# A decoder layer on one core: the last head's scaling on ScalarE, the residual rows on SP's queue, the first up weight's low parts on VectorE, the second up weight's splits moved within the token chains

## The chip, the core and the metric

The kernel runs on one core of one Trainium2 chip. The core has five engines that work side by side, each through its own instructions in order: TensorE (PE, matmuls), VectorE (DVE), ScalarE (ACT), GpSimd (POOL), and SyncE (SP), which here only issues DMAs. ACT issues DMAs too, and such an issue stands in ACT's queue like any other instruction. The metric is the device time of one execution in microseconds (us).

## What is computed

One layer of a decoder, for 512 tokens of 1024 numbers, in float32. Cut to what matters here:

```python
u = rms_norm(x, mix_pre_g) * (1.0 + sc1) + sh1        # sh, sc, g: six rows from cond @ ada_w + ada_b
h = mlstm_chunkwise(...)                              # 4 heads x 256
h = rms_norm(h, ml_norm_g) * sigmoid(o_pre)           # per head
y = silu(layer_norm(causal_dwconv(a * sigmoid(gt))))  # convolution group
mix = jnp.concatenate([h, y], axis=-1) @ w_out
x = x + g1 * rms_norm(mix, mix_post_g)
u = rms_norm(x, ffn_pre_g) * (1.0 + sc2) + sh2
up = causal_dwconv(u @ ffn_up)                        # 2 x 2816 columns
a, gt = jnp.split(up, 2, axis=-1)
f = (silu(gt) * a) @ ffn_down
x = x + g2 * rms_norm(f, ffn_post_g)
```

## The kernel before

Every large product is made of three matmuls (`mm3`): each operand is split into a high part, rounded by a copy on ACT (L191), and a low part, the difference, by a subtraction on POOL or DVE (L192). `w_split` does this for one 128x512 piece of a weight, `w_load` for a whole load of 1 MB, which is four pieces. Weights come through two buffers (`raws`, RAWS = 2): SP can issue a load only when the splits of the load before last have read their buffer. Split pieces live in `wpool` (20 tiles, ten pieces) or in `slots`.

The order on PE and SP is that of the program. ACT, DVE and POOL are ordered by a scheduler, except inside `in_order()`, where they too run in program order. The queue of each engine is then fixed: an instruction that waits holds up all behind it.

The part of the program that the change touches runs from the last head's attention to the first up products:

- **The last head** (`attention(3)`). For each of four token tiles PE makes a bank `o`; ACT reads from it the denominator (`dm`, L545), copies it to `hn` (L546) and sums its squares (L547). Then DVE and POOL make four columns `rd` and `fac` (L552 to L557), DVE scales the four pieces of `hn` by both (L560), PE transposes them (`hT`, L566), and DVE and ACT make from them the high and low parts `hh`, `hl` that the output projection reads.
- **The first half of the output projection** (`mix_first`, banks `mixa`), of which 10 of 16 steps stand ahead of hT and 6 behind it, and then the first 8 steps of the second half (banks `mixb`, one for each token tile).
- **The modulation** (`ada_block`, L174 to L176). Loads of 512 KB on ACT's queue, each multiplied and summed by DVE. Sixteen of them run behind the last head, through six buffers (four in `spare`, two in `adas`). They end in `gains` (L931 to L933), which PE transposes (`gT`, L665); DVE copies the result to `gTs` (L667), and SP sends it to memory and reads it back as rows for all partitions (`gs2r`, `sh2r`).
- **The residual** `x1`: eight tiles of x, 256 KB each, loaded on ACT's queue (L921) into buffers that the convolution group has used.
- **The token chains**, inside `in_order()` (L1013 to L1049). For each token tile: `mix_last` ends its `mixb` bank; `chain_sums` squares it on ACT, multiplies it on DVE (L948) and makes a factor on DVE and POOL; `chain_x` adds it to `x1` (L955), squares the sum and makes the next factor; `chain_u` ends the normalised tile `un` (L963); `turn_tile` transposes it on PE (`xT`, L971); `turn_out` splits it into `u2h`, `u2l`. Then come the first products of the feed-forward part (`up_half`). Between these steps stand single pieces of the second and third up weight (`up_split`), whose low parts are made on DVE.

The names in the views: `wo` is a piece of the output weight, `wup` one of an up weight, and `wup_0`, `_512`, `_1024`, `_1536` are its four pieces; `h` and `l` at the end are the high and the low part.

Of the kernel before, what the change touches and what calls it, by code (L numbers as in the profile page):

```python
# [13 lines left out]
AF = mybir.ActivationFunctionType  # L14
ALU = mybir.AluOpType
# [4 lines left out]
T = 512  # L20
KT = D // P
NT = T // P
H = 4
# [32 lines left out]
def decoder_layer(ctx, tc, w_glu0, x, c, adaT, vecs, w_glu, w_qko, w_v0, w_v, w_out, w_up, w_down, out):  # L56
    nc = tc.nc
    V, S, G, PE = nc.vector, nc.scalar, nc.gpsimd, nc.tensor

    const = ctx.enter_context(tc.tile_pool(name="const", bufs=1))  # L60
    slots = ctx.enter_context(tc.tile_pool(name="slots", bufs=SLOTS))
# [123 lines left out]
    def w_split(src, name, pool=None, tag="w", eng=None):  # L185

        n = src.shape[1]
        pool = pool or wpool
        hi = pool.tile([P, T], F32R, tag=tag, name=f"{name}h")
        lo = pool.tile([P, T], F32R, tag=tag, name=f"{name}l")  # L190
        S.activation(hi[:, :n], src, AF.Copy)  # L191
        (eng or G).tensor_tensor(out=lo[:, :n], in0=src, in1=hi[:, :n].bitcast(F32), op=ALU.subtract)  # L192
        return hi, lo

    def w_load(view, name, pool=None, tag="w"):

        n = view.shape[1]
        r = raws.tile([P, 2048], F32, tag="raw", name=name)
        nc.sync.dma_start(r[:, :n], view)
        return [w_split(r[:, a : min(a + T, n)], f"{name}_{a}", pool, tag) for a in range(0, n, T)]  # L200

    def blk(pieces, b):
        hi, lo = pieces[b // 4]
# [109 lines left out]
    _, _, u = u_tiles("u")  # L313
# [209 lines left out]
    def attention(h):  # L523

        _, qs, ks, so = heads[h]

        for cc in range(NT):
            n = NS[cc]
            sp = atbank(f"s{h}_{cc}")
            for d in range(2):  # L530
                PE.matmul(sp[:, :n], ks[d][:, cc * P : (cc + 1) * P], qs[d][:, cc * P :], start=d == 0, stop=d == 1)  # L531
            last_e[0] = V.scalar_tensor_tensor(out=E[h][cc], in0=sp[:, :n], scalar=DH**-0.5, in1=E[h][cc], op0=ALU.mult, op1=ALU.mult)
            if cc in ((0, 2, 3) if h == 0 else (1, 3)):
                yield
        ssq = small.tile([P, NT], F32, tag="ssq", name=f"ssq{h}")
        dm = small.tile([P, NT], F32, tag="dm", name=f"dm{h}")
        hn = [slot(f"hn{h}_{i}") for i in range(2)]
        for tt in range(NT):
            o = atbank(f"o{h}_{tt}")
            for cc in range(tt + 1):  # L540
                a = (tt - cc) * P
                PE.matmul(o[:, : DH + 2], E[h][cc][:, a : a + P], vs[h][cc], start=cc == 0, stop=cc == tt)  # L542
            junk = small.tile([P, DH], BF16, tag="junk2", bufs=1, name=f"junko{h}_{tt}")
            hv = hn[tt // 2][:, (tt % 2) * DH : (tt % 2 + 1) * DH]
            S.activation(dm[:, tt : tt + 1], o[:, DH : DH + 1], AF.Abs)  # L545
            S.activation(hv, o[:, :DH], AF.Copy)  # L546
            S.activation(junk, hv, AF.Square, accum_out=ssq[:, tt : tt + 1])  # L547
            if tt in (1, 2):
                yield
        rd = small.tile([P, NT], F32, tag="rd", name=f"rd{h}")  # L550
        fac = small.tile([P, NT], F32, tag="fac", name=f"fac{h}")
        V.tensor_tensor(out=dm, in0=dm, in1=em[:, :, h], op=ALU.max)  # L552
        V.reciprocal(rd, dm)
        V.scalar_tensor_tensor(out=ssq, in0=ssq, scalar=1.0 / DH, in1=rd, op0=ALU.mult, op1=ALU.mult)
        V.tensor_tensor(out=ssq, in0=ssq, in1=rd, op=ALU.mult)
        G.tensor_scalar(out=ssq, in0=ssq, scalar1=EPS, scalar2=None, op0=ALU.add)
        G.tensor_tensor(out=fac, in0=ssq, in1=mhalf, op=ALU.pow)  # L557
        for tt in range(NT):
            hv = hn[tt // 2][:, (tt % 2) * DH : (tt % 2 + 1) * DH]
            V.tensor_scalar(out=hv, in0=hv, scalar1=fac[:, tt : tt + 1], scalar2=rd[:, tt : tt + 1], op0=ALU.mult, op1=ALU.mult)  # L560
        yield
        for e in range(2):
            tp = atbank(f"hT{h}_{e}")
            for tt in range(NT):
                src = hn[tt // 2][:, (tt % 2) * DH + e * P : (tt % 2) * DH + (e + 1) * P]
                PE.transpose(tp[:, tt * P : (tt + 1) * P], src, ident)  # L566
            t = so[e]
            V.scalar_tensor_tensor(out=t, in0=t, scalar=1.0, in1=tp, op0=ALU.add, op1=ALU.mult)
            hi, lo = slot(f"hh{h}_{e}", F32R), slot(f"hl{h}_{e}", F32R)
            g = ghalf[:, 2 * h + e : 2 * h + e + 1]  # L570
            S.activation(hi, t, AF.Copy, scale=g)
            last_lo[0] = V.scalar_tensor_tensor(out=lo, in0=t, scalar=g, in1=hi.bitcast(F32), op0=ALU.mult, op1=ALU.subtract)
            hy[2 * h + e] = (hi, lo)
# [128 lines left out]
    def tok(tt):  # L702
        return slice(tt * P, (tt + 1) * P)
# [6 lines left out]
    def wo_rows(hf, g):  # L710
        return w_load(w_out[hf, g], f"wo{hf}_{g}")
# [203 lines left out]
    x1 = side_parts("x1_0") + side_parts("x1_1")  # L915
    x1 = [x1[2 * tt : 2 * tt + 2] for tt in range(NT)]
    wide1 = vpool.tile([P, 2 * T + 8], F32, tag="vh", name="g1r")
    g1r = row(0, lambda n: [wide1[:, :T], wide1[:, T : 2 * T]], "g1")
    for tt in range(NT):
        for hf in range(2):  # L920
            nc.scalar.dma_start(x1[tt][hf], x[tok(tt), hf * T : (hf + 1) * T])  # L921
    for tt, ps in enumerate(mixa):
        V.tensor_tensor(out=mg[tt], in0=ps, in1=g1r[0], op=ALU.mult)
        sq_sum(ps, msq[:, 2 * tt : 2 * tt + 1], f"mixa{tt}")
# [7 lines left out]
    S.activation(gains[:, 2 * KT : 3 * KT], sc2[:, :, 1], AF.Copy)  # L932
    S.activation(gains[:, KT : 2 * KT], gains[:, KT : 2 * KT], AF.Copy, scale=RD)  # L933
    wo = [w for g in range(KA // 4, 4) for w in wo_rows(1, g)]

    HT = T // 2
    u2h = upool.tile([P, 2, KT, HT], F32R, tag="uh", name="u2h")
# [4 lines left out]
    def chain_sums(tt):  # L942

        ps = banks[tt]
        sq_sum(ps, msq[:, 2 * tt + 1 : 2 * tt + 2], f"mixb{tt}")
        un = adas.tile([P, D], F32, tag="ada", name=f"un{tt}")
        uns[tt] = [un[:, :T], un[:, T:]]
        V.tensor_tensor(out=uns[tt][1], in0=ps, in1=g1r[1], op=ALU.mult)  # L948
        return token_factor(msq[:, 2 * tt : 2 * tt + 2], f"rm{tt}")

    def chain_x(tt, r):

        xsq = small.tile([P, 2], F32, tag="xsq", name=f"xsq{tt}")
        for hf, m in enumerate((mg[tt], uns[tt][1])):
            V.scalar_tensor_tensor(out=x1[tt][hf], in0=m, scalar=r, in1=x1[tt][hf], op0=ALU.mult, op1=ALU.add)  # L955
            sq_sum(x1[tt][hf], xsq[:, hf : hf + 1], f"x1_{tt}_{hf}")
        for hf, un in enumerate(uns[tt]):
            V.tensor_tensor(out=un, in0=x1[tt][hf], in1=gs2r[hf], op=ALU.mult)
        return token_factor(xsq, f"rf{tt}")

    def chain_u(tt, r):
        for hf, un in enumerate(uns[tt]):
            V.scalar_tensor_tensor(out=un, in0=un, scalar=r, in1=sh2r[hf], op0=ALU.mult, op1=ALU.add)  # L963
# [17 lines left out]
    def mix_last(tt, a, b):  # L981
        for n_, k in enumerate(MIX[KA:]):
            if a <= n_ < b:
                mm3(banks[tt], (hy[k][0][:, tok(tt)], hy[k][1][:, tok(tt)]), wo[n_], False, n_ == 2 * KT - KA - 1)
# [7 lines left out]
    def up_split(i, r, pool, tag):  # L992
        q = len(up_w[i])
        up_w[i].append(w_split(r[:, q * T : (q + 1) * T], f"wup{i}_{q * T}", pool, tag, V))
# [8 lines left out]
            for k in range(KT):  # L1003
                mm3(ps[:, th * HT : (th + 1) * HT], blk(up_w[i], half * KT + k), (u2h[:, th, k, :], u2l[:, th, k, :]), k == 0, k == KT - 1)

    up_w = {0: w_load(w_up[0], "wup0", slots, "t")}
    send_rows(KT, 2 * KT, nc.sync)
    gs2r = row(1, cvtile, "gs2", nc.sync)
    sh2r = row(2, cvtile, "sh2", nc.sync)
    raw1 = raw_up(1)  # L1010
    raw2 = raw_up(2)
    early += [[mmbank(f"up{i}_{half}") for half in range(2)] for i in range(2)]
    with in_order():  # L1013
        for tt in range(3):
            mix_last(tt, 0, 2 * KT - KA)
        up_split(1, raw1, slots, "t")
        r = chain_sums(0)
        up_split(1, raw1, slots, "t")
        r = chain_x(0, r)
        chain_u(0, r)  # L1020
        turn_tile(0)
        mix_last(3, 0, 7)
        r = chain_sums(1)
        up_split(1, raw1, slots, "t")
        r = chain_x(1, r)
        chain_u(1, r)
        turn_out(0)
        turn_tile(1)
        mix_last(3, 7, 2 * KT - KA)
        r = chain_sums(2)  # L1030
        turn_out(1)
        r = chain_x(2, r)
        up_split(1, raw1, slots, "t")
        chain_u(2, r)
        up_half(0, 0)
        turn_tile(2)
        r = chain_sums(3)
        up_split(2, raw2, wpool, "w")
        r = chain_x(3, r)
        up_split(2, raw2, wpool, "w")  # L1040
        chain_u(3, r)
        up_half(0, 1)
        up_split(2, raw2, wpool, "w")
        early.append([cvbank(f"up2_{half}") for half in range(2)])
        up_half(0, 2, 0)
        turn_tile(3)
        turn_out(2)
        up_split(2, raw2, wpool, "w")
        turn_out(3)  # L1049
# [57 lines left out]
    for i in range(NF):  # L1107
# [21 lines left out]
        a = conv3(pa, i, f"fa{i}")  # L1129
# [222 lines left out]
```

## Time and profile before

| | us |
|---|---|
| median of three runs | 777.75 |
| lowest and highest of them | 775.51, 778.12 |
| the profiled execution | 778.95 |
| its span, first to last instruction | 777.2 |

All views come from that one execution; their times count from the start of its span. A row of a timeline gives start, duration, engine, line, operation, what is written and read, and in brackets the idle time ahead of it and what ended it. DMA-issuing instructions have the engine name ACTq or SPq and do not count as busy time. The page's time line, in 40 slices of 19.4 us with tenths of busy time, shows PE nearly always busy:

```
PE   8999999999999999999998999999999999999996
DVE  6679999979499775669918798675765677664548
ACT  6685438675656455562225444434444345566633
POOL 4789759895656663445441558886988786599943
DMA  8964214213032161585742765766586574796363
```

### The profile page before, as it was taken

The page shows a single profiled execution, that of the slowest core. Times are in us where ns is not written, and L with a number is a line of the kernel's source. Part 1 is how long each engine was busy: PE and PEld are TensorE (multiplying, and loading weights), DVE is VectorE, ACT ScalarE, POOL GpSimd, SP SyncE. Part 2 cuts the span into 40 slices and gives each one's busy share as a digit, 9 for nine tenths or more (in the row PEclk, how much of TensorE's full clock was granted, in tenths as well). Part 3 has the DMA queues.
Part 4 walks back from the last instruction along what each step waited for, and adds up shares of the span by engine and source line. Part 5 has one row for each costly group of instructions (what it writes and reads, how often), then busy time and mean ns, then how long its engine had stood idle before and what let it go on. Part 6 is the DMA issues. An engine that isn't in the chain of part 4 may idle for free.

```text
span 777.2 us, 10579 instructions
## 1 busy us (share of the span) xinstructions
PE 762.8 (98%) x3706; PEld 639.1 (82%) x3706; DVE 574.0 (74%) x830; ACT 407.7 (52%) x770; POOL 526.6 (68%) x436
## 2 busy tenths in 40 slices
PE   8999999999999999999998999999999999999996
PEld 6788898878888888887886998888888888888885
DVE  6679999979499775669918798675765677664548
ACT  6685438675656455562225444434444345566633
POOL 4789759895656663445441558886988786599943
PEclk9999999999999999999999999999999999999999
DMA  8964214213032161585742765766586574796363
GB/s 319 356 263 137 82 55 163 82 51 139 28 94 96 55 213 59 190 280 178 299 163 82 247 218 186 277 235 246 204 304 224 216 291 149 272 398 242 109 233 147
DMA packets 40570, 147.36 MB, mean 190 GB/s; under 512 B 3874, under 2 KB 5314, under 8 KB 31300
## 3 DMA queue, kind: packets, MB, share of 16 engines
q1 hardware_dynamic: 25652, 92.40, 33.4%
q10 hardware_dynamic: 14864, 54.28, 19.3%
q8 instruction: 29, 0.48, 0.2%
q14 instruction: 25, 0.20, 0.1%
HBM read 126.59 MB, written 20.07 MB: 189 GB/s over the span
## 4 chain that ended last, share of the span: by engine, by line
PE 85%; DVE 4%; DMA 4%; ACT 2%; POOL 2%; issue 2%; ACTq 1%; SPq 0%; DVEq 0%; POOLq 0%
PE up L210 31%; PE qko L210 17%; PE dn L210 9%; PE glu L210 7%; PE v L210 6%; PE mixb L210 4%; PE mixa L210 2%; PE s L531 2%; PE o L542 2%; PE glu L356 2%; DMA p<-spill_t 1%; DMA wup<-in_w_up 1%; DMA wglu<-in_w_glu 1%; DMA ada<-in_adaT 1%; DVE hn L560 1%
## 5 line engine op out<-in xcount | busy, mean ns | idle before, releaser
L747 DVE SCALAR_TENSOR_TENSOR cv<-gt,cvw,cv 128x485 f32<-128x485 f32 (+23 forms) x200 | 137.0, 729 | 2.7 <-ACT cv L735 1.3
L743 POOL TENSOR_TENSOR cs<-cs,cs 128x510 f32<-128x510 f32 (+3 forms) x32 | 41.7, 1306 | 0.1
L210 PE MATMUL up<-u2l,wup_0h 128*128 128x512 f32 (+1 forms) x100 | 36.5, 365 | 0.2 <-DVE u2l L979 0.2
L210 PE MATMUL up<-u2h,wup_0h 128*128 128x512 f32 (+1 forms) x100 | 36.5, 365 | 0.0
L210 PE MATMUL up<-u2h,wup_1024h 128*128 128x512 f32 (+1 forms) x100 | 36.4, 364 | 0.0
L210 PE MATMUL up<-u2h,wup_0l 128*128 128x512 f32 (+1 forms) x100 | 36.4, 364 | 0.0
L210 PE MATMUL up<-u2l,wup_1536h 128*128 128x512 f32 (+1 forms) x100 | 36.4, 364 | 0.0
L210 PE MATMUL up<-u2l,wup_512h 128*128 128x512 f32 (+1 forms) x100 | 36.4, 364 | 0.0
L210 PE MATMUL up<-u2h,wup_1024l 128*128 128x512 f32 (+1 forms) x100 | 36.4, 364 | 0.0
L210 PE MATMUL up<-u2h,wup_1536h 128*128 128x512 f32 (+1 forms) x100 | 36.4, 364 | 0.0
L210 PE MATMUL up<-u2h,wup_512h 128*128 128x512 f32 (+1 forms) x100 | 36.4, 364 | 0.0
L210 PE MATMUL up<-u2h,wup_512l 128*128 128x512 f32 (+1 forms) x100 | 36.4, 364 | 0.0
L210 PE MATMUL up<-u2h,wup_1536l 128*128 128x512 f32 (+1 forms) x100 | 36.4, 364 | 0.0
L210 PE MATMUL up<-u2l,wup_1024h 128*128 128x512 f32 (+1 forms) x100 | 36.4, 364 | 0.0
L192 POOL TENSOR_TENSOR wup_0l<-wup,wup_0h 128x512 fp32r<-128x512 f32 x20 | 30.6, 1529 | 4.5 <-ACT wup_0h L191 4.5
L176 DVE SCALAR_TENSOR_TENSOR junk<-ada,cb 128x1024 bf16<-128x1024 f32 x20 | 29.6, 1479 | 5.4 <-DMA ada<-in_adaT 5.3
L192 POOL TENSOR_TENSOR wup_1024l<-wup,wup_1024h 128x512 fp32r<-128x512 f32 x20 | 26.3, 1317 | 8.3 <-ACT wup_1024h L191 8.3
L192 POOL TENSOR_TENSOR wup_1536l<-wup,wup_1536h 128x512 fp32r<-128x512 f32 x20 | 29.0, 1449 | 4.4 <-ACT wup_1536h L191 4.2
L741 ACT ACTIVATE cs<-gt,cvw 128x511 f32<-128x511 f32 (+4 forms) x40 | 27.2, 712 | 5.1 <-POOL cs L743 3.4
L1086 DVE TENSOR_TENSOR b<-b 128x512 f32<-128x512 f32 x11 | 19.4, 1762 | 11.3 <-POOL b L1085 11.3
L192 POOL TENSOR_TENSOR wup_512l<-wup,wup_512h 128x512 fp32r<-128x512 f32 x20 | 27.5, 1377 | 0.0
L1085 POOL TENSOR_TENSOR b<-b 128x512 f32<-128x512 f32 x11 | 14.2, 1289 | 16.0 <-DVE b L1084 16.0
(1058 smaller groups left out, 2784.9 us busy)
## 6 DMA issues: line engine op xcount, KB each, us to landing
wup<-in_w_up SPq DMA_DIRECT2D x22, 1024.0 KB, 5.5
wqko<-in_w_qko SPq DMA_DIRECT2D x12, 1024.0 KB, 4.8
b<-in_w_down ACTq DMA_DIRECT2D x11, 1024.0 KB, 5.0
spill_t<-b ACTq DMA_DIRECT2D x11, 1024.0 KB, 4.9
ada<-in_adaT ACTq DMA_DIRECT2D x20, 512.0 KB, 6.0
ada<-in_adaT SPq DMA_DIRECT2D x16, 512.0 KB, 7.1
wo<-in_w_out SPq DMA_DIRECT2D x8, 1024.0 KB, 6.4
spare<-in_adaT ACTq DMA_DIRECT2D x12, 512.0 KB, 5.9
```

What stands on the lines that cost most here:

```text
L176: t = V.scalar_tensor_tensor(out=junk, in0=r, scalar=1.0, in1=cb, op0=ALU.mult, op1=ALU.mult, accum_out=mod[:, i : i + 1])
L192: (eng or G).tensor_tensor(out=lo[:, :n], in0=src, in1=hi[:, :n].bitcast(F32), op=ALU.subtract)
L210: PE.matmul(ps, l, r, start=start and i == 0, stop=stop and i == 2, skip_group_check=again)
L356: PE.matmul(ps, blk(wk, i)[a], u[k][b], start=k == 0 and p == 0, stop=k == KT - 1 and p == 1)
L531: PE.matmul(sp[:, :n], ks[d][:, cc * P : (cc + 1) * P], qs[d][:, cc * P :], start=d == 0, stop=d == 1)
L542: PE.matmul(o[:, : DH + 2], E[h][cc][:, a : a + P], vs[h][cc], start=cc == 0, stop=cc == tt)
L560: V.tensor_scalar(out=hv, in0=hv, scalar1=fac[:, tt : tt + 1], scalar2=rd[:, tt : tt + 1], op0=ALU.mult, op1=ALU.mult)
L741: S.activation(t[:, d:], cvx[j][:, : T - d], AF.Copy, scale=w(CK - 1 - d))
L743: G.tensor_tensor(out=side[:, d:], in0=side[:, d:], in1=t[:, d:], op=ALU.add)
L747: tap = V.scalar_tensor_tensor(out=cp[:, d:], in0=cvx[j][:, : T - d], scalar=w(CK - 1 - d), in1=cp[:, d:], op0=ALU.mult, op1=ALU.add)
L1085: G.tensor_tensor(out=b12, in0=b22, in1=b12, op=ALU.subtract)
L1086: V.tensor_tensor(out=b22, in0=b22, in1=b11, op=ALU.subtract)
```

## The change

Four edits. First, for the last head alone, DVE multiplies `fac` by `rd` once (128x4), and the four pieces of `hn` are scaled by that product on ACT. Second, the eight loads of `x1` are issued by SP, behind the last load of the output weight, in place of ACT. Third, `w_load` takes an engine, and the low parts of the first up weight are made on DVE in place of POOL. Fourth, the first two pieces of the second up weight stand behind the squares of the token chains: the first behind `chain_x(0)` in place of ahead of `chain_sums(0)`, the second ahead of `chain_x(1)`, the third behind it; the fourth stays.

```diff
-    def w_load(view, name, pool=None, tag="w"):
+    def w_load(view, name, pool=None, tag="w", eng=None):
...
-        return [w_split(r[:, a : min(a + T, n)], f"{name}_{a}", pool, tag) for a in range(0, n, T)]
+        return [w_split(r[:, a : min(a + T, n)], f"{name}_{a}", pool, tag, eng) for a in range(0, n, T)]
...
         G.tensor_tensor(out=fac, in0=ssq, in1=mhalf, op=ALU.pow)
+        if h == H - 1:
+            V.tensor_tensor(out=fac, in0=fac, in1=rd, op=ALU.mult)
         for tt in range(NT):
             hv = hn[tt // 2][:, (tt % 2) * DH : (tt % 2 + 1) * DH]
+            if h == H - 1:
+                S.activation(hv, hv, AF.Copy, scale=fac[:, tt : tt + 1])
+                continue
             V.tensor_scalar(out=hv, in0=hv, scalar1=fac[:, tt : tt + 1], scalar2=rd[:, tt : tt + 1], op0=ALU.mult, op1=ALU.mult)
...
     g1r = row(0, lambda n: [wide1[:, :T], wide1[:, T : 2 * T]], "g1")
-    for tt in range(NT):
-        for hf in range(2):
-            nc.scalar.dma_start(x1[tt][hf], x[tok(tt), hf * T : (hf + 1) * T])
...
     wo = [w for g in range(KA // 4, 4) for w in wo_rows(1, g)]
+    for tt in range(NT):
+        for hf in range(2):
+            nc.sync.dma_start(x1[tt][hf], x[tok(tt), hf * T : (hf + 1) * T])
...
-    up_w = {0: w_load(w_up[0], "wup0", slots, "t")}
+    up_w = {0: w_load(w_up[0], "wup0", slots, "t", V)}
...
     with in_order():
         for tt in range(3):
             mix_last(tt, 0, 2 * KT - KA)
+        r = chain_sums(0)
+        r = chain_x(0, r)
         up_split(1, raw1, slots, "t")
-        r = chain_sums(0)
-        up_split(1, raw1, slots, "t")
-        r = chain_x(0, r)
         chain_u(0, r)
         turn_tile(0)
         mix_last(3, 0, 7)
         r = chain_sums(1)
         up_split(1, raw1, slots, "t")
         r = chain_x(1, r)
+        up_split(1, raw1, slots, "t")
         chain_u(1, r)
```

What stands in the queues. ACT's queue at the end of the last head's attention, before (`dm`, `hn` and `junko` with `o_3` are the fourth token tile; `x_1` is the second half of the residual; a row ending in x4 is four instructions):

```order
L545 ACTIVATE dm_3391<-o_2_3443 128x1
L546 ACTIVATE hn_1_3393<-o_2_3443 128x256
L547 ACTIVATE junko_2_3447,ssq_3390<-hn_1_3393 128x256
L921 DMA x_1_3712<-in_x 128x512 x4
L191 ACTIVATE wo_0_0h<-wo_0_3740 128x512
L545 ACTIVATE dm_3391<-o_3_3463 128x1
L546 ACTIVATE hn_1_3393<-o_3_3463 128x256
L547 ACTIVATE junko_3_3468,ssq_3390<-hn_1_3393 128x256
L191 ACTIVATE wo_0_512h<-wo_0_3740 128x512
L191 ACTIVATE wo_0_1024h<-wo_0_3740 128x512
L191 ACTIVATE wo_0_1536h<-wo_0_3740 128x512
```

The same place of ACT's queue now:

```order
L545 ACTIVATE dm_3391<-o_2_3443 128x1
L546 ACTIVATE hn_1_3393<-o_2_3443 128x256
L547 ACTIVATE junko_2_3447,ssq_3390<-hn_1_3393 128x256
L191 ACTIVATE wo_0_0h<-wo_0_3733 128x512
L545 ACTIVATE dm_3391<-o_3_3463 128x1
L546 ACTIVATE hn_1_3393<-o_3_3463 128x256
L547 ACTIVATE junko_3_3468,ssq_3390<-hn_1_3393 128x256
L191 ACTIVATE wo_0_512h<-wo_0_3733 128x512
L563 ACTIVATE hn_0_3392<-hn_0_3392,fac_3473 128x256 x2
L563 ACTIVATE hn_1_3393<-hn_1_3393,fac_3473 128x256 x2
L191 ACTIVATE wo_0_1024h<-wo_0_3733 128x512
L191 ACTIVATE wo_0_1536h<-wo_0_3733 128x512
```

The four DMA issues are gone from between the third and the fourth tile, and the four scalings stand behind one weight piece and ahead of two.

DVE's queue from the gTs copy to the end of the first token tile's chain, before (`wup_0l` and `wup_512l` belong to the second up weight):

```order
L667 COPY gTs_3933<-gT_3931 16x128
L192 TENSOR_TENSOR wup_0l<-wup_3945,wup_0h 128x512
L948 TENSOR_TENSOR un_4031<-mixb_3736,g1r 128x512
L697 TENSOR_SCALAR rm0t<-msq 128x1
L192 TENSOR_TENSOR wup_512l<-wup_3945,wup_512h 128x512
L955 SCALAR_TENSOR_TENSOR x_0_3711<-mg_3707,rm0r,x_0_3711 128x512
L955 SCALAR_TENSOR_TENSOR x_0_3711<-un_4031,rm0r,x_0_3711 128x512
L958 TENSOR_TENSOR un_4031<-x_0_3711,gs2r_3937 128x512
L958 TENSOR_TENSOR un_4031<-x_0_3711,gs2r_3938 128x512
L697 TENSOR_SCALAR rf0t<-xsq_4041 128x1
L963 SCALAR_TENSOR_TENSOR un_4031<-un_4031,rf0r,sh2r_3941 128x512
L963 SCALAR_TENSOR_TENSOR un_4031<-un_4031,rf0r,sh2r_3942 128x512
```

The same stretch now (`wup_3914` is the first up weight, of whose four pieces the last is shown; `wup_3946` is the second):

```order
L192 TENSOR_TENSOR wup_1536l<-wup_3914,wup_1536h 128x512
L672 COPY gTs_3934<-gT_3932 16x128
L953 TENSOR_TENSOR un_4028<-mixb_3729,g1r 128x512
L702 TENSOR_SCALAR rm0t<-msq 128x1
L960 SCALAR_TENSOR_TENSOR x_0_3712<-mg_3708,rm0r,x_0_3712 128x512
L960 SCALAR_TENSOR_TENSOR x_0_3712<-un_4028,rm0r,x_0_3712 128x512
L963 TENSOR_TENSOR un_4028<-x_0_3712,gs2r_3938 128x512
L963 TENSOR_TENSOR un_4028<-x_0_3712,gs2r_3939 128x512
L702 TENSOR_SCALAR rf0t<-xsq_4034 128x1
L192 TENSOR_TENSOR wup_0l<-wup_3946,wup_0h 128x512
L968 SCALAR_TENSOR_TENSOR un_4028<-un_4028,rf0r,sh2r_3942 128x512
L968 SCALAR_TENSOR_TENSOR un_4028<-un_4028,rf0r,sh2r_3943 128x512
```

The second up weight's first piece has moved from ahead of the chain to the place ahead of its last two steps, its second piece has left this stretch, and the first up weight's four pieces have come in ahead of the copy.

## The prediction

> **What bounds it.** I read the page first, then TensorE's waits, then TensorE's instructions in order of time around each wait. The page, span and busy times:
>
> ```profile
> span 777.2 us, 10579 instructions
> PE 762.8 (98%) x3706; PEld 639.1 (82%) x3706; DVE 574.0 (74%) x830; ACT 407.7 (52%) x770; POOL 526.6 (68%) x436
> ```
>
> TensorE (PE) is busy for 762.8 of 777.2 us and the diff leaves its instructions alone. So the change can only return PE's idle time, or time in which PE runs slowly. Its waits for other engines from 300 us on, in all, times, longest:
>
> ```profile
> PE xT L971 <- DVE un L963: 2.3, 1, 2.3
> PE hT L566 <- DVE hn L560: 1.6, 2, 1.0
> PE xT L971 <- DVE un L948: 0.6, 1, 0.6
> PE up L210 <- DVE u2l L979: 0.2, 1, 0.2
> ```
>
> Three of the four are at the places that the change touches: the transposes of the last head's output (hT) and those of the first token tile (xT). PE's timeline there (start, duration):
>
> ```profile
> 352.31 0.27 PE L566 MATMUL hT<-ident,hn 128*128 128x128 f32 x1
> 353.15 0.33 PE L566 MATMUL hT<-ident,hn 128*128 128x128 f32 x1 [0.57 <-DVE hn L560]
> 354.51 1.09 PE L566 MATMUL hT<-ident,hn 128*128 128x128 f32 x6 [1.04 <-DVE hn L560]
> ...
> 398.84 0.39 PE L210 MATMUL mixb<-wo_1536l,yh 128*128 128x512 f32 x1
> ...
> 399.29 0.39 PE L210 MATMUL mixb<-wo_0h,yh 128*128 128x512 f32 x1
> ...
> 409.95 0.39 PE L210 MATMUL mixb<-wo_1536h,yl 128*128 128x512 f32 x1
> 412.67 0.66 PE L971 MATMUL xT<-ident,un 128*128 128x128 f32 x4 [2.33 <-DVE un L963]
> 413.93 0.66 PE L971 MATMUL xT<-ident,un 128*128 128x128 f32 x4 [0.61 <-DVE un L948]
> 414.34 0.62 PE L210 MATMUL mixb<-wo_0h,yh 128*128 128x512 f32 x1
> ...
> 418.07 0.39 PE L210 MATMUL mixb<-wo_1536h,yh 128*128 128x512 f32 x1
> ```
>
> A matmul normally starts every 0.225 us (two steps from 398.84 to 399.29). Behind the second wait, nine take 418.07 - 414.34 = 3.73 us, 0.41 each. The windows view gives the clock there (last three columns: granted clock, DMA share, GB/s):
>
> ```profile
> 352.00:356.00 4.00, 2.40 (x14) 1.55 (x13) 3.58 (x5) 0.70 (x2) 2.21 (x2) 1.00 0.14 27
> 414.30:418.00 3.70, 3.70 (x12) 2.92 (x11) 3.08 (x6) 1.88 (x6) 0.80 (x2) 0.54 0.36 132
> ```
>
> So the wait at 410 to 414 us costs twice: once as idle time and once as 3.7 us at a clock of 0.54. The shorter hT waits left the clock at 1.00.
>
> **Edit 1: scaling on ScalarE (ACT), x1 loads off its queue.** What hT waits for:
>
> ```profile
> 342.36 1.91 PE L542 MATMUL o<-v,E 128*128 128x258 f32 x8
> 343.02 3.05 ACTq L921 DMA_DIRECT2D x<-in_x  x4
> 346.72 0.15 ACT L545 ACTIVATE dm<-o 128x1 f32<-128x1 f32 x1
> 346.89 1.29 POOL L192 TENSOR_TENSOR wo_0l<-wo,wo_0h 128x512 fp32r<-128x512 f32 x1 [4.45 <-ACT dm L545]
> 346.90 1.30 DVE L552 TENSOR_TENSOR dm<-dm,em 128x4 f32<-128x4 f32 x1 [3.91 <-ACT dm L545]
> 349.35 1.04 POOL L557 TENSOR_TENSOR fac<-ssq,mhalf 128x4 f32<-128x4 f32 x1
> 350.42 4.36 DVE L560 TENSOR_SCALAR hn<-hn,fac,rd 128x256 f32<-128x256 f32 x4 [1.55 <-POOL fac L557]
> L546 ACT ACTIVATE hn<-o 128x256 f32<-128x256 f32 x4 | 1.5, 368 | 0.0
> ```
>
> The fourth o bank is done at 344.27, but ACT reads it only at 346.72, since four DMA issues hold its queue for 3.05 us. Without them ACT reads it at once, 2.4 us earlier. The factor, ready at 350.39 now, then comes at 348.0. The added DVE product of two 128x4 tiles is bounded by 0 and by the 1.30 us that L552, the same form, took beside GpSimd (POOL); I take 0.2, since POOL's next subtraction comes only behind ACT's next piece. Four ACT scalings are priced by L546, the same shape on ACT: 4 x 0.37 = 1.5 us, against 4.36 on DVE. They are ready at 348.0 + 0.2 + 1.5 = 349.7, or 350.8 by the upper bound; PE arrives at 352.31. Behind them in ACT's queue stand two weight pieces that wait for PE anyway. Both hT waits go: **-1.6 us**. Everything behind on PE moves up by 1.6.
>
> **Edit 2: eight x1 loads on SP's queue.**
>
> ```profile
> x<-in_x ACTq DMA_DIRECT2D x8, 256.0 KB, 7.6
> ...
> 368.00:378.00 10.00, 10.00 (x46) 8.29 (x45) 9.90 (x15) 3.03 (x8) 4.27 (x3) 1.00 1.02 382
> ...
> 387.02 1.23 DVE L176 SCALAR_TENSOR_TENSOR junk<-spare,cb 128x1024 bf16<-128x1024 f32 x1
> ...
> 388.49 0.21 ACT L932 ACTIVATE gains<-mod 128x8 f32<-128x8 f32 x1 [7.74 <-DVE mod L181]
> ```
>
> They now stand behind the last output weight's load and ahead of the first up weight's. Their own wait is over by then: the last four were issued at 343.02, so their tiles were free. The move puts 2 MB into a stretch that already moves 382 GB/s: 5.4 us of transfer at that rate. The modulation loads run beside them, and their last user on DVE ends at 388.25. Between nothing and 5.4 us of delay I take nothing: DVE keeps six such loads in flight and has no idle time in those rows' stretch (9.90 of 10 us busy). The upper bound goes into a rival.
>
> **Edit 3: the first up weight's low parts on DVE.**
>
> ```profile
> 394.01 0.28 DVE L667 COPY gTs<-gT 16x128 f32<-16x128 f32 x1 [5.35 <-PE gT L665]
> 396.81 1.28 POOL L192 TENSOR_TENSOR wo_1536l<-wo,wo_1536h 128x512 fp32r<-128x512 f32 x1
> ```
>
> POOL's last output piece ends at 398.09, and PE uses it at 398.84. With PE 1.6 us earlier, 0.85 us of edit 1 would be lost here. Taking four 1.3 us subtractions out of POOL's queue ahead of it removes that; I count it as zero, not as a gain. The price is that DVE's four pieces now stand ahead of the gTs copy, which PE allows at 394.01 - 1.6 = 392.4. ACT reaches gains at 386.9; six more of its steps at up to 0.64 (the row of wup_0h below) bring the last high part to 390.7, DVE's last piece (0.69, the last row below) to 391.4. The margin is 1.0 us; beyond it the copy, and with it the rows and the second weight's load that SP issues behind it, come late one to one. The Trainium skill, "SBUF — State Buffer", section "Who interferes with whom", says that a DVE instruction with two SBUF inputs and a GpSimd instruction lock each other out for a whole instruction. The trace agrees: L552's 1.30 us end with POOL's subtraction at 348.2. One such lock would make the copy 0.3 us late.
>
> **Edit 4: the second up weight's splits behind the tile's squares.**
>
> ```profile
> 397.42 7.85 DMA wup<-in_w_up
> 405.29 0.64 ACT wup_0h L191
> ...
> 406.56 0.68 DVE L948 TENSOR_TENSOR un<-mixb,g1r 128x512 f32<-128x512 f32 x1
> 411.86 1.41 DVE L963 SCALAR_TENSOR_TENSOR un<-un,rf0r,sh2r 128x512 f32<-128x512 f32 x2 [0.66 <-POOL rf0r L699]
> 413.19 0.68 DVE L948 TENSOR_TENSOR un<-mixb,g1r 128x512 f32<-128x512 f32 x1
> 418.47 1.41 DVE L963 SCALAR_TENSOR_TENSOR un<-un,rf1r,sh2r 128x512 f32<-128x512 f32 x2 [0.66 <-POOL rf1r L699]
> 426.38 0.69 DVE L192 TENSOR_TENSOR wup_1536l<-wup,wup_1536h 128x512 fp32r<-128x512 f32 x1 [0.31 <-ACT wup_1536h L191]
> ```
>
> Tile 0's bank is complete at about 399.5 (tile 1's first matmul starts at 399.29), but its chain stands in order behind a weight that lands at 405.27: 5.8 us lost. Afterwards tile 0 starts at 397.9. ACT's square (0.6) and the 5.30 us from 406.56 to 411.86 bring it to its last step at 403.8. That step now waits for the weight's first piece instead: landing 405.27 - 1.6 = 403.7, + 0.64 + 0.69 = 405.0, + 1.41 = 406.4. PE wants it at 410.34 - 1.6 = 408.7, so the waits of 2.33 and 0.61 go, with 2.3 us to spare. On ACT the waiting high part now has tile 1's square behind it, which is done by 403.7 + 0.64 + 0.8 = 405.1, before DVE gets to tile 1.
>
> Then tile 1. Its chain took 419.88 - 413.19 = 6.7; one piece now stands ahead of its last step, 0.31 + 0.69 - 0.66 = 0.34 more by tile 2's row. Ready at 406.4 + 7.0 = 413.4. PE arrives at 408.6 + 0.87 (eight transposes) + 21 x 0.225 = 414.2. The margin is 0.8: this is the next wait to come. Tile 2 and what follows have the same order as before.
>
> ```profile
> 428.72 0.87 PE xT L971 x8
> ```
>
> Gain: from 409.95 to 414.34 are 4.39 us, unstalled 0.225 + 0.87 = 1.10, so 3.29. The nine slow matmuls: 3.73 - 9 x 0.225 = 1.70. Together **-5.0 us**.
>
> **Sum.** 1.6 + 5.0 = 6.6. The profiled execution took 778.95 us (the span and 1.75 around it): 772.35. The median of the runs shown is 1.2 below it, so 777.75 - 6.6 = **771.2** there.
>
> **Rivals.** (a) The wait moves to tile 1. If the weight lands, or gTs is copied, more than 0.8 us later than worked out, xT of tile 1 waits. For: the margin, and two loads of 1 MB now issued together. Against: SP no longer waits for POOL's last piece before the second. Price 0.3 to 1.3, and 1.7 more if the clock falls: 771.5 to 774.2, centre 773. Chance 0.15.
>
> (b) The slow clock is not the stall's. By this mechanism the nine matmuls stay slow: 771.2 + 1.7 = 772.9. Against it: 0.54 stands right behind the longest wait. The Trainium skill, "TensorE: Matmul & The Clock Gate", Part 1, has the clock halved only after an idle window of about 3.4 us. The trace shows the fall after 2.33 and 0.61 us idle with four transposes between, so it does not bear out that length as idle time. Chance 0.03.
>
> (c) Edit 1 does not do what it says: the scalings come late in ACT's queue and hT still waits 1.6: 772.8. Against: 1.5 us of margin even at the upper bound. Chance 0.03.
>
> (d) The lead is lost later: the feed-forward part waits for weights and only edit 1 is left, 776.1. Against: PE's waits list nothing after 422.84, and the loads there are released by steps that move along. Chance 0.06.
>
> (e) Slower: the x1 loads hold up the modulation or the first up weight, and with it the gTs copy, on which rows and second weight hang. Tile 0 is then ready 14.0 us behind the copy (394.01 to 405.27, then 2.74). Up to a copy at 393.2 nothing shows; from there the loss is one to one. The gain is gone at 399.8, and at 403.0 the time is 781. That is 10.6 us behind 392.4; the 2 MB make 5.4. Chance 0.05.
>
> **Numbers.** Forecast 0.68, (a) 0.15, (b) 0.03, (c) 0.03, (d) 0.06, (e) 0.05. About 0.3% (2.3 us) is what a measurement of this kernel can tell from no change. Faster: all but (d) and (e), less some scatter, 0.87; same 0.08; slower 0.05. Range: the runs lie from 2.2 below to 0.4 above their median, so 771.2 - 2.2 = 769.0 below; above, (a)'s end with scatter, 774.2 + 0.4 = 774.6.
>
> **What would show it.** Right: no wait of hT, none of xT of tile 0, clock 1.00 around 408 to 414 us, the scalings on ACT done before 351, chain_u of tile 0 released by wup_0l and not by POOL. Wrong: a wait of xT of tile 1, a gTs copy well after 392.4 with an idle time ended by ACT's up pieces, waits of PE after 425, or DVE idle for modulation loads between 365 and 388.

## The result, and the profile after

The changed kernel takes 773.75 us (median of 8 runs, 772.82 to 775.99), the kernel before, run beside it, 777.74 (8 runs, 775.51 to 780.41). The ratio is 0.9953, 95% interval 0.9935 to 0.9971: faster by half a per cent. The forecast was 771.2, with a range of 769.0 to 774.6, so the sign and the range are right and the number is 2.5 us too low. The profiled execution took 772.87 us, the second shortest of those eight. Its page, span and busy times:

```profile
span 771.1 us, 10583 instructions
PE 760.4 (99%) x3706; PEld 637.3 (83%) x3706; DVE 567.0 (74%) x831; ACT 411.0 (53%) x774; POOL 520.8 (68%) x432
```

PE's busy time fell only from 762.8 to 760.4 us while the span fell by 6.1, so most of what went is idle time. PE's waits from 300 us on, four rows before, are now one, and it is a new one:

```profile
PE xT L976 <- DVE u2l L984: 0.7, 1, 0.7
```

PE's timeline at the places shown before (the last row is the first product of the feed-forward part), and the windows of the first two tiles (granted clock, DMA share and GB/s are the last three columns):

```profile
352.60 1.03 PE L571 MATMUL hT<-ident,hn 128*128 128x128 f32 x8
391.72 0.27 PE L670 MATMUL gT<-ident,gains 128*16 128x128 f32 x1
...
408.20 1.03 PE L976 MATMUL xT<-ident,un 128*128 128x128 f32 x8
414.67 1.25 PE L976 MATMUL xT<-ident,un 128*128 128x128 f32 x8 [0.65 <-DVE u2l L984]
416.46 0.28 PE L210 MATMUL up<-u2h,wup_0h 128*128 128x256 f32 x1
```

```profile
410.00:414.00 4.00, 4.00 (x18) 3.00 (x16) 3.69 (x8) 3.26 (x9) 0.54 (x1) 1.00 0.35 131
414.00:418.00 4.00, 3.35 (x23) 2.75 (x23) 3.94 (x9) 1.19 (x2) 0.54 (x1) 1.00 0.00 0
```

hT runs as one group of eight, tile 0's xT too, the clock is 1.00 throughout, and the only idle time is 0.65 us, ahead of tile 1's xT. The last head, now:

```profile
342.65 1.91 PE L542 MATMUL o<-v,E 128*128 128x258 f32 x8
344.66 0.38 ACT L546 ACTIVATE hn<-o 128x256 f32<-128x256 f32 x1
347.51 0.16 DVE L559 TENSOR_TENSOR fac<-fac,rd 128x4 f32<-128x4 f32 x1 [1.54 <-POOL fac L557]
347.72 1.70 ACT L563 ACTIVATE hn<-hn,fac 128x256 f32<-128x256 f32 x4
```

ACT reads the fourth bank (L546) 2.01 us after that group of matmuls begins (4.41 before), and the scalings end at 349.4, 3.2 us ahead of PE. The copy of the scale row, and tile 1's chain:

```profile
387.92 1.21 DVE L933 SCALAR_TENSOR_TENSOR gains<-mod,vec 128x8 f32<-128x8 f32 x1
390.45 1.37 DVE L192 TENSOR_TENSOR wup_0l<-wup,wup_0h 128x512 fp32r<-128x512 f32 x1 [1.32 <-ACT wup_0h L191]
...
392.95 0.68 DVE L192 TENSOR_TENSOR wup_1536l<-wup,wup_1536h 128x512 fp32r<-128x512 f32 x1
393.55 0.27 DVE L672 COPY gTs<-gT 16x128 f32<-16x128 f32 x1
...
405.13 0.69 DVE L192 TENSOR_TENSOR wup_0l<-wup,wup_0h 128x512 fp32r<-128x512 f32 x1 [2.57 <-ACT wup_0h L191]
405.74 1.41 DVE L968 SCALAR_TENSOR_TENSOR un<-un,rf0r,sh2r 128x512 f32<-128x512 f32 x2
...
412.61 1.41 DVE L968 SCALAR_TENSOR_TENSOR un<-un,rf1r,sh2r 128x512 f32<-128x512 f32 x2
413.94 1.28 DVE L984 TENSOR_TENSOR u2l<-xT,u2h 128x512 fp32r<-128x512 f32 x2
```

gT is on PE at 391.72, and before, the copy followed gT by 0.31 us (393.70 to 394.01). Now it comes 1.83 behind, since DVE's four low parts stand ahead of it. Tile 1's `un` is ready at 414.02. But PE waits for the u2l of tile **0** (413.94): both halves of xT share two banks, so tile 1's transposes overwrite tile 0's, and DVE must have read those first. On DVE that reading stands behind tile 1's last step.

### The profile page after: what moved, and what is told of

Read it like the earlier page. It is cut to its first block, busy times and chain, and to the rows that moved or that the text cites. A ratio compares the mean times of both kernels' runs of the same rounds, so it can differ in the third digit from the quotient of the medians.

```text
span 771.1 us, 10583 instructions
## 1 busy us (share of the span) xinstructions
PE 760.4 (99%) x3706; PEld 637.3 (83%) x3706; DVE 567.0 (74%) x831; ACT 411.0 (53%) x774; POOL 520.8 (68%) x432
## 4 chain that ended last, share of the span: by engine, by line
PE 86%; DVE 4%; DMA 4%; ACT 2%; issue 2%; POOL 1%; SPq 0%; DVEq 0%; ACTq 0%; POOLq 0%
PE up L210 31%; PE qko L210 16%; PE dn L210 12%; PE glu L210 7%; PE v L210 6%; PE mixa L210 5%; PE o L542 2%; PE s L531 2%; PE glu L356 2%; DMA x<-in_x 1%; DMA wup<-in_w_up 1%; DMA spare<-in_adaT 1%; DMA wglu<-in_w_glu 1%; POOL wglu_0l L192 0%; PE cps L159 0%
## 5 line engine op out<-in xcount | busy, mean ns | idle before, releaser
L192 POOL TENSOR_TENSOR wqko_1024l<-wqko,wqko_1024h 128x512 fp32r<-128x512 f32 x12 | 15.5, 1293 | 18.4 <-PE v L210 10.3
L192 POOL TENSOR_TENSOR wo_1024l<-wo,wo_1024h 128x512 fp32r<-128x512 f32 x8 | 11.4, 1421 | 21.7 <-ACT wo_1024h L191 16.4
```

## The experiments

The runs are compared by marks in their traces, because executions of one kernel differ. "Last o" is the start of PE's last eight o matmuls, ahead of everything that the change touches. "hT ends" is the end of the eighth transpose. "Rest" is the span less that. "Copy" is the start of gTs less that of gT. All in us, one profiled execution each:

| kernel | span | last o | hT ends | rest | waits of xT, tile 0 / 1 | copy |
|---|---|---|---|---|---|---|
| before | 777.2 | 342.36 | 355.60 | 421.6 | 2.33 + 0.61 / 0 | 0.31 |
| before, 2nd | 777.0 | 344.92 | 356.31 | 420.7 | 1.62 + 0.60 / 1.16 | 0.31 |
| before, 3rd | 777.4 | 341.99 | 355.69 | 421.7 | 1.53 + 0.60 / 1.17 | 0.30 |
| splits undone | 777.7 | 342.54 | 353.52 | 424.2 | 4.31 / 0 | 2.06 |
| changed | 771.1 | 342.65 | 353.63 | 417.5 | 0 / 0.65 | 1.83 |
| changed, 2nd | 770.9 | 342.42 | 353.40 | 417.5 | 0 / 0.58 | 2.18 |
| changed, 3rd | 770.0 | 341.79 | 352.77 | 417.2 | 0 / 0.40 | 1.03 |
| x1 on ACT | 772.2 | 343.93 | 354.91 | 417.3 | 0 / 0.41 | 2.06 |
| x1 late on SP | 772.1 | 343.48 | 354.46 | 417.6 | 0 / 0.76 | 1.39 |
| scaling on DVE | 774.5 | 344.40 | 355.39 | 419.1 | 0.59 / 1.40 | 2.51 |
| splits only | 772.1 | 344.22 | 355.48 | 416.6 | 0 / 0 | 0.31 |
| splits only, 2nd | 770.5 | 342.76 | 353.81 | 416.7 | 0 / 0 | 0.31 |
| low parts on POOL | 770.2 | 342.55 | 353.53 | 416.7 | 0 / 0 | 0.31 |
| low parts on POOL, split later | 771.8 | 344.24 | 355.22 | 416.6 | 0 / 0 | 0.31 |

The rest falls into three groups: 420.7 to 424.2 with the splits ahead of tile 0's chain; 417.2 to 417.6, once 419.1, with edits 3 and 4; 416.6 to 416.7 with edit 4 and without edit 3.

**The changed kernel as a base**, no edit.

> The changed kernel once more, as the yardstick on this chip. All theories: span 770 to 773, no wait of hT, a wait of xT of the second token tile of about 0.65, ratio to before 0.994 to 0.997.

773.42 us, 0.994 (0.9917 to 0.9963), with tile 1's wait again (0.58).

> The changed kernel once more, as the base of the three runs beside it. Theory: hT ends at 353.5 us where PE's start-up waits are short (0.3 us) and as much later as these are longer; tile 0 without a wait, tile 1's xT waits 0.4 to 0.8 us; span 770.9 to 772, time 772.7 to 773.8.

On another chip 773.55, 0.9956 (0.9939 to 0.9972), tile 1's wait 0.40. The span, 770.0, lies 0.9 under the low end expected, with the earliest last o of all.

**The fourth edit alone**, the kernel before with

```diff
-        up_split(1, raw1, slots, "t")
         r = chain_sums(0)
-        up_split(1, raw1, slots, "t")
         r = chain_x(0, r)
+        up_split(1, raw1, slots, "t")
         chain_u(0, r)
...
         r = chain_x(1, r)
+        up_split(1, raw1, slots, "t")
```

> The kernel before with the fourth edit alone. Forecast's theory: the waits of xT of the first tile (2.33 and 0.61) and the slow clock behind them go, worth 5.0; hT still waits 1.6; the second tile's chain is ready 0.8 ahead of PE, so xT waits nowhere: span 777.2 - 5.0 = 772.2. Rival 'slow clock is not the stall's': nine matmuls at 0.41 stay, span 773.9. Rival 'the second tile always waits': xT of the second tile waits 0.5 or more, as in the changed kernel, span 772.8.

772.7 us, 0.9943 (0.9918 to 0.9967): the whole gain that can be measured. Tile 0's waits and the low clock are gone, and the expected hT wait isn't there either.

> The kernel before with the fourth part alone, once more. Theory: its turn of the last head ends at 355.5 to 356.3 us in every execution, by a wait of hT on hn where PE came early and without one where PE lost the time ahead, so its span is 772 to 773 and its time 0 to 2 us above the changed kernel's: whatever PE's start-up does, the residual rows on ACT's queue and the scaling on VectorE set that end. Rival (the first part is worth nothing): its span and time lie within 0.5 us of the changed kernel's, or below.

772.55 us beside the changed kernel's 773.55 on the same chip; 0.9936 (0.9922 to 0.995). The theory fell: hT ended at 353.81, not at 355.5 or later, and span and time lie where the rival put them. Its last head:

```profile
342.76 1.91 PE L542 MATMUL o<-v,E 128*128 128x258 f32 x8
343.53 1.79 ACTq L921 DMA_DIRECT2D x<-in_x  x4
...
349.67 3.33 DVE L560 TENSOR_SCALAR hn<-hn,fac,rd 128x256 f32<-128x256 f32 x4 [1.55 <-POOL fac L557]
...
352.71 1.10 PE L566 MATMUL hT<-ident,hn 128*128 128x128 f32 x8
```

The same four DMA issues took 1.79 us here and 3.05 in before's profile, and the scalings ended 10.24 us behind the last o instead of 12.42. PE comes 9.95 behind it and takes the pieces one by one, so all that shows is a turn of 1.10 us instead of 1.03.

**The kernel before, twice more**, no edit.

> The kernel before once more, unchanged, to see what of its waits belongs to the kernel and what to one execution. Theory of the forecast: PE's wait at the last head's turn (hT on hn) is about 1.6 us in every execution, tile 0's wait (xT on un) 2 to 3 us with a granted clock well under 1 in the 4 us behind it; from PE's first hT to the first matmul of the up projection 70 us. Rival, after the splits-only run: the hT wait comes and goes (0 to 1.6 us) with the time that ACT's issues of the residual rows take (2.0 to 3.05 us for four), tile 0's wait and the low clock stay, and the stage takes 68.5 to 70 us.

> As for the run before it: the kernel before, a third execution. If the hT wait differs by over 0.5 us between the three executions, the rival holds; if all three have 1.4 to 1.8 us, the forecast's theory holds and the splits-only run was the odd one.

The hT wait was 0 in the second execution (the turn took 1.44 us instead of 1.03) and 1.6 in the third, with DMA issues of 2.12 and 3.15 us: it comes and goes, as the rival said. But the low clock isn't in every execution behind tile 0 either, as both theories had it: it is in neither of these two. From hT's start to the first product they took 67.45 and 70.83 us, outside the rival's 68.5 to 70. The third:

```profile
352.84 0.33 PE L566 MATMUL hT<-ident,hn 128*128 128x128 f32 x1 [0.63 <-DVE hn L560]
354.14 1.55 PE L566 MATMUL hT<-ident,hn 128*128 128x128 f32 x6 [0.97 <-DVE hn L560]
...
413.11 0.66 PE L971 MATMUL xT<-ident,un 128*128 128x128 f32 x4 [1.53 <-DVE un L963]
414.37 0.66 PE L971 MATMUL xT<-ident,un 128*128 128x128 f32 x4 [0.60 <-DVE un L948]
420.99 1.26 PE L971 MATMUL xT<-ident,un 128*128 128x128 f32 x8 [1.17 <-DVE u2l L979]
```

```profile
354.00:358.00 4.00, 3.86 (x12) 3.15 (x13) 3.27 (x7) 1.45 (x2) 0.00 (x0) 0.58 0.74 262
...
414.00:416.00 2.00, 1.63 (x9) 1.44 (x10) 1.57 (x4) 0.00 (x0) 0.92 (x1) 1.00 0.04 8
```

Here the clock fell behind hT (0.58), and stayed at 1.00 behind tile 0. With PE at full speed there, tile 1's xT waits 1.17 us for tile 0's u2l, the wait that the changed kernel has. In the first profile PE was slow in that stretch, came later to tile 1, and the wait didn't show. The three spans are 777.0 to 777.4 either way: in these executions the end of this stage was set by the chain behind the copy and the second up weight, not by PE's speed.

**Edits 1 to 3 without the fourth**, the changed kernel with the two `up_split` lines ahead of `chain_x(0)` again.

> The changed kernel with its fourth part undone: the first two splits of the second up weight stand ahead of tile 0's chain again. Forecast's sum: the hT wait gone (-1.6), tile 0's wait and low clock back, so about 776.2 us against 777.8. Rival (the hT wait belongs to some executions only): between 0 and -1 us, 776.8 to 777.8, and tile 0's wait with a low clock in its profile. If the time is below 775, the splits' place isn't what the gain hangs on.

779.09 us, beside 778.78 for the kernel before on that chip; 0.9997 (0.9976 to 1.0017): nothing is gained, about as the rival said.

```profile
352.49 1.03 PE L571 MATMUL hT<-ident,hn 128*128 128x128 f32 x8
412.55 2.38 PE L976 MATMUL xT<-ident,un 128*128 128x128 f32 x8 [4.31 <-DVE un L968]
```

```profile
414.00:416.00 2.00, 2.00 (x7) 1.72 (x7) 1.57 (x3) 0.25 (x1) 0.87 (x1) 0.50 0.03 8
```

hT ends 2.1 us earlier than before, and tile 0 begins at 412.55, as before (412.67). The lead becomes waiting time: 4.31 us, and a longer low clock behind it. 1.75 us of it are lost already at the copy (2.06 behind gT instead of 0.31).

**The residual rows put elsewhere**: in the first run their issues are back on ACT's queue (L921), in the second on SP behind the first up weight's load.

```diff
-    for tt in range(NT):
-        for hf in range(2):
-            nc.sync.dma_start(x1[tt][hf], x[tok(tt), hf * T : (hf + 1) * T])
...
     up_w = {0: w_load(w_up[0], "wup0", slots, "t", V)}
+    for tt in range(NT):
+        for hf in range(2):
+            nc.sync.dma_start(x1[tt][hf], x[tok(tt), hf * T : (hf + 1) * T])
```

> The changed kernel with the x1 loads back on ACT at their old place. Theory 'x1 loads hold up the modulation': with them gone from there, DVE does not wait 2.0 us for the last modulation load, the copy to gTs comes at 392.0 to 392.7 and not at 393.55, and the second tile's xT wait (0.65) goes; hT waits 0 to 0.4, since the factor is ready only at 350.4 but the scaling on ACT takes 1.7: span 770.4 to 770.9, not slower than the changed kernel. Rival 'the four pieces on DVE hold up the copy': copy at 393.2 or later, the 0.65 stays, span 771.3. Rival 'the move to SP is what freed hT': hT waits 1 us or more, span 772 or more.

> The changed kernel with the x1 loads on SP behind the first up weight's load. Theory 'x1 loads hold up the modulation': no wait of DVE for the last modulation load, copy to gTs at 392.0 to 392.7, no wait of the second tile, no wait of hT: span 770.3, 0.6 to 0.9 below the changed kernel. Rival 'the four pieces on DVE hold up the copy': copy at 393.2 or later, xT of the second tile still waits 0.3 or more, span 770.8 to 771.1. Rival 'x1 comes too late there': the first tile's sums wait for x1 or SP is still issuing at 393.6, and xT of the first or second tile waits over 1 us, span 772 or more.

773.86 (0.9948, 0.9931 to 0.9964) and 773.28 (0.9931, 0.9906 to 0.9955): neither differs from the changed kernel. In both the copy is still late and tile 1 still waits, so it doesn't take the rows on SP ahead of the up weight to make the copy late. The second one's DVE and POOL:

```profile
389.94 0.68 DVE L192 TENSOR_TENSOR wup_512l<-wup,wup_512h 128x512 fp32r<-128x512 f32 x1
390.54 1.78 DVE L192 TENSOR_TENSOR wup_1024l<-wup,wup_1024h 128x512 fp32r<-128x512 f32 x1
392.24 1.78 DVE L192 TENSOR_TENSOR wup_1536l<-wup,wup_1536h 128x512 fp32r<-128x512 f32 x1
393.94 0.27 DVE L672 COPY gTs<-gT 16x128 f32<-16x128 f32 x1
```

```profile
390.35 1.42 POOL L192 TENSOR_TENSOR wo_1024l<-wo,wo_1024h 128x512 fp32r<-128x512 f32 x1 [0.88 <-ACT wo_1024h L191]
391.73 1.74 POOL L192 TENSOR_TENSOR wo_1536l<-wo,wo_1536h 128x512 fp32r<-128x512 f32 x1
```

A subtraction of one shape takes 0.68 us on DVE alone and 1.78 beside POOL's subtractions, which stretch too. The Trainium skill, "SBUF — State Buffer", section "Who interferes with whom", has the two lock each other out for whole instructions when the DVE one has two SBUF inputs and the GpSimd one reads SBUF. These rows agree: the two slow pieces end at 392.32 and 394.02, each 0.55 us behind the POOL piece that it met (391.77 and 393.47). The two such locks cost 2.2 us ahead of the copy.

**The first up weight's low parts on POOL**, the changed kernel without its third edit:

```diff
-    up_w = {0: w_load(w_up[0], "wup0", slots, "t", V)}
+    up_w = {0: w_load(w_up[0], "wup0", slots, "t")}
```

> The changed kernel with its third part undone: the first up weight's low parts on POOL again. Theory (the four pieces on VectorE, locked against POOL's subtractions, hold up the copy of the scale row): the copy gTs comes within 0.5 us of PE's gT, the chain of tile 0 is bounded by the landing of the second up weight alone, tile 1's xT wait at most 0.2 us, stage from the first hT to the first up matmul about 63.2 us, time 0 to 0.6 us below the changed kernel's. Rival (the residual rows on SP's queue hold up the last modulation columns and with them the copy): copy still over 1 us behind gT and tile 1's wait 0.4 us or more.

772.55 us, 0.9923 (0.9896 to 0.995). The theory held in each point that the trace shows, with x1 still on SP; its point on the time stays open, as the changed kernel was not run on that chip:

```profile
391.62 0.27 PE L670 MATMUL gT<-ident,gains 128*16 128x128 f32 x1
413.77 1.15 PE L976 MATMUL xT<-ident,un 128*128 128x128 f32 x8
415.46 0.28 PE L210 MATMUL up<-u2h,wup_0h 128*128 128x256 f32 x1
```

```profile
391.93 0.28 DVE L672 COPY gTs<-gT 16x128 f32<-16x128 f32 x1 [2.81 <-PE gT L670]
412.93 1.28 DVE L984 TENSOR_TENSOR u2l<-xT,u2h 128x512 fp32r<-128x512 f32 x2
```

PE has no wait left from 300 us on. From hT's start (352.50) to the first product are 62.96 us, 63.86 in the changed kernel.

**The last head's scaling on VectorE**, the changed kernel without the first half of edit 1 (the four `hn` scalings on DVE, as in the other heads).

> The changed kernel with the last head's scaling on VectorE again and the residual rows still on SP. Theory (the rows' issues on ACT's queue, not the scaling's engine, made the last head late): scalings end near 351 to 352 us, PE's hT waits at most 0.3 us and ends at 353.5 to 354, time within 0.5 us of the changed kernel's. Rival (the scaling under POOL's lock is the last to come): hT waits 0.5 to 1.5 us and ends at 355 or later.

```profile
349.27 2.47 DVE L560 TENSOR_SCALAR hn<-hn,fac,rd 128x256 f32<-128x256 f32 x4 [1.55 <-POOL fac L557]
354.36 1.03 PE L566 MATMUL hT<-ident,hn 128*128 128x128 f32 x8
418.01 1.26 PE L971 MATMUL xT<-ident,un 128*128 128x128 f32 x8 [1.40 <-DVE u2l L979]
```

The theory held for hT: the scalings end at 351.7, 2.6 us before PE, so with the DMA issues off ACT's queue either engine does. hT ended at 355.39, not at 353.5 to 354 as expected, because PE itself was late (last o at 344.40). The time, 774.24 (0.995, 0.993 to 0.997), has an interval too wide to part it from 773.55. Its copy was the latest of all (2.51), and with it came the longest wait at tile 1.

**Low parts on POOL, and the first split one place later**, behind the sums of tile 1:

```diff
         r = chain_x(0, r)
-        up_split(1, raw1, slots, "t")
         chain_u(0, r)
...
         r = chain_sums(3)
+        up_split(1, raw1, slots, "t")
         up_split(2, raw2, wpool, "w")
```

> The changed kernel with the third part undone and the second up weight's splits moved one place further: the first one behind the sums of tile 1 in place of ahead of tile 0's last step. Theory: the chain of tile 0 no longer waits for that weight's landing (404 us) and ends near 403 to 405, tile 1's chain 2 us earlier than the changed kernel's, so its xT doesn't wait and has over 1 us in hand; PE had no other wait there, so the time is that of the run with the low parts on POOL, 0 to 1 us below the changed kernel's. Rival (a later split is late somewhere else): a new wait of the up projection's matmuls on its low parts, and a time above the changed kernel's.

771.93 us, 0.9933 (0.9916 to 0.9949), the lowest median of all and 1.6 below the changed kernel's on the same chip, where 0 to 1 was expected, though the two intervals overlap.

```profile
404.82 1.41 DVE L968 SCALAR_TENSOR_TENSOR un<-un,rf0r,sh2r 128x512 f32<-128x512 f32 x2 [0.66 <-POOL rf0r L704]
...
412.27 1.41 DVE L968 SCALAR_TENSOR_TENSOR un<-un,rf1r,sh2r 128x512 f32<-128x512 f32 x2
```

Tile 0's last step is released by its own factor and no longer by the weight. It ends at 406.23, later than the 403 to 405 expected, as this execution's copy came at 393.62 and not at 391.9. Tile 1 is ready at 413.68, 1.8 us before PE (415.46). Nothing new waits.

## Why the forecast was right, and where it was wrong

**Edit 4, 5.0 us: right in size.** "Splits only" has a rest of 416.6 and 416.7 us against 421.6 in the profile that the sum was made from: 4.9 to 5.0 (against the second execution of before, 4.0 to 4.1). The 1.70 for the slow matmuls was part of the stall, so rival (b) fell: no run without a wait at tile 0 shows a low clock there. But the split into 3.29 idle and 1.70 slow belongs to that one execution; in the two others the clock stayed up there and tile 1 waited 1.2 instead.

**Edit 1, 1.6 us: right mechanism, wrong as a constant.** Without the DMA issues, ACT copies from the last bank 2.0 us behind the last o in every run, with them 3.25 to 4.47. But PE waits only where the issues take 3 us: in two of the five executions of before and of splits only. hT ends 10.98 or 10.99 us behind the last o in all nine executions with this edit, whole or in part, and 11.05 to 13.70 in the five without: it is worth 0.1 to 2.7 us there, and 2.26 in the profile that the sum was made from, where 1.6 counted the waits alone and not the transposes that ran apart between them. With the rows' issues left on ACT ("x1 on ACT") nothing was in hand: the added product met a subtraction on POOL and took 1.25 us, near its bound of 1.30, and the scalings ended 9.92 us behind the last o, where PE came at 9.95. The gain counts only if nothing behind it takes the lead back, as "splits undone" shows. In the timed medians this edit's part can't be told from nothing.

**Edit 3, counted as zero with 1.0 us of margin: wrong.** The forecast weighed one meeting of DVE with POOL. In the changed kernel's profile there were three ahead of the copy: two steps that make the scale columns, L181 and L933, took 1.15 and 1.21 us instead of 0.17 each, and the first low part 1.37 instead of 0.68. ACT reached gains at 387.92 instead of 386.9, and the copy came 1.15 behind the 392.4 worked out. All seven executions with this edit have the copy 0.7 to 2.2 us later than the seven without; with edit 4, their rest is 0.5 to 1.0 us longer, once 2.5. What it was to save (0.85 for POOL's last output piece) isn't missed: no wait of PE on it shows in the runs without it. In the times the edit's loss can't be told from nothing either.

**"The margin is 0.8: this is the next wait to come": the place was right, the condition was not.** It looked at tile 1's `un` alone. The banks of xT must also have been read by tile 0's u2l, which DVE reaches only when that `un` is done, some 0.6 us later still. With the late copy, rival (a) came true on top of the forecast: 0.40 to 0.76 us, and 1.40 once. Before's first profile did not show this wait, but the program's order could, and the list of waits showed one of its kind: tile 0's 0.61 us, ended by L948, is PE waiting for DVE to read tile 1's `mixb`, whose bank the second half of xT overwrites.

**Edit 2, counted as nothing: not quite.** All seven executions with the rows on SP ahead of the up weight have DVE waiting for a modulation load between 365 and 388 us, 0.2 to 2.9 us in all, and none of the other seven has. The changed kernel's profile, and below it a row of "x1 late on SP", where only the rows' place differs:

```profile
385.26 1.44 DVE L176 SCALAR_TENSOR_TENSOR junk<-spare,cb 128x1024 bf16<-128x1024 f32 x1 [2.03 <-DMA spare<-in_adaT]
...
385.58 2.27 POOL L192 TENSOR_TENSOR wo_512l<-wo,wo_512h 128x512 fp32r<-128x512 f32 x1
...
386.74 1.15 DVE L181 TENSOR_TENSOR mod<-mod,vec 128x16 f32<-128x16 f32 x1
```

```profile
387.15 0.18 DVE L181 TENSOR_TENSOR mod<-mod,vec 128x16 f32<-128x16 f32 x1
```

DVE reaches the sum behind these waits (L181) 43.0 to 44.8 us after the last o there and 43.7 to 47.0 in the others: no later. But in all seven the sum and the next step (L933) meet POOL and take 1.14 to 1.15 and 1.20 to 1.21 us, and in the other seven 0.17 or 0.18: with the rows there ACT makes wo_512h ahead of gains, in the others behind it, so POOL has subtractions left beside these steps. The two steps are some 2 us longer by that. Alone this costs nothing: in "low parts on POOL" the copy is on time. It is part of what used up edit 3's margin. Rival (e) at its price did not come. Rivals (c) and (d) fell too: no hT wait, and nothing lost behind the first product.

**The step that cost 2 of the 2.5 us: the base.** Against its own execution the sum gave 778.95 - 6.6 = 772.35; the profile after took 772.87. That this is only 0.5 more is in part luck: the last o came 0.3 later and 0.8 to 0.9 were lost at tile 1, but edit 1 gave 0.65 more than counted. Then "The median of the runs shown is 1.2 below it, so 777.75 - 6.6" took a gain read from one execution off the middle of others, as if it were a constant. The two profiled executions are 6.1 apart, but the first lay above its kernel's median and the second is the second shortest of its eight; the medians are 4.0 apart, and 4.4 and 3.8 in the two repeats.

Why the gain is smaller in the middle stays open. In the three profiles of before the last o comes between 341.99 and 344.92, and the span is 777.0 to 777.4 all the same. Of the 2.56 us that PE came later in the second than in the first, the hT wait took up all but 0.7, and the second up weight's load the rest (7.16 us from its issue to its first use instead of 7.87). In the changed kernel nothing takes it up: span less last o is 428.5, 428.5 and 428.2. By that the gain would be 777.2 - 771.1 = 6.1 where PE is early, and 777.0 - 344.92 - 428.4 = 3.7 where it is as late as 344.92. But the timed runs, which left no trace, do not bear this out. If before took up what PE lost, its times should lie closer together than the changed kernel's; side by side, before's spread over 4.9, 6.2 and 4.6 us, the changed kernel's over 3.2, 2.4 and 5.4. And the shortest times of the two kernels are only 2.7 to 4.0 apart. What makes PE late ahead of the last head (waits of 0.2 to 1.8 us at the start, 1.4 at `o` in one run) was not tried.

## What to carry to other kernels

A wait that a profile shows can belong to that execution: here the same wait at hT was 1.6, 0 and 1.6 us in three executions of one kernel. So profile the kernel twice or three times before a wait's length goes into a sum, and don't take a gain read from one execution off the median of others. For a margin behind a moved step, list everything that its consumer waits for, the readers of the buffer that it overwrites included. And before work is moved from an idle engine to another, look at what stands behind it in that engine's queue: here a copy of 0.3 us on which a megabyte of weights hung.

## What the runs showed of the hardware

Four DMA issues of 256 KB on ACT's queue took 1.79 to 3.15 us, by execution, and held up the whole queue. The second up weight's first piece could start on ACT 7.0 to 8.4 us after SP had issued the load. The clock fell behind waits of 2.33 + 0.61 us (0.54) and 4.31 us (0.50), and stayed at 1.00 behind 1.53 + 0.60 and 1.62 + 0.60; but of two nearly equal waits at hT, 0.57 + 1.04 left it at 1.00 and 0.63 + 0.97 lowered it to 0.58. So the length of a wait doesn't say whether it costs twice. Nor does the whole stretch in which PE has only transposes: 3.2 us at the hT that slowed down, and 3.3 and 3.2 at the two tiles that did not. Shorter windows show what the three slow stretches have in common: the clock was 0.50 for 3.4 us (354.6 to 358.0 in the third execution of before, 414.5 to 417.9 in the first) or twice as long (411.7 to 418.5 in "splits undone"). That suggests a clock set in steps of 3.4 us with a beat of its own, by which the same wait can fall well or badly; no run here tests that.
